# Two more projections by Strassen's seven products, with the residual kept token by token

## The chip, the cores and the metric

The kernel runs on one core of a Trainium2 chip. The core has a matrix engine (TensorE, PE in the profile), a vector engine (VectorE, DVE), an engine for activation functions and copies (ScalarE, ACT), GpSimd (POOL) and SyncE (SP), which here only issue transfers, and 16 DMA engines. Matmuls write PSUM, which has eight banks of 128 x 512 floats; all else lies in SBUF. The metric is the time of one execution on the device in microseconds (us).

## The reference

One layer of a decoder on 512 tokens of width 1024, all in float32, with 256 memory tokens:

```
h = x
h = h + hybrid_mixer(rmsnorm(h, mix_norm), ...)
h = h + memory_cross_attention(rmsnorm(h, xattn_norm), rmsnorm(mem, mem_norm), w_q, w_kv, w_o)
h = h + swiglu(rmsnorm(h, ffn_norm), w_gate_up, w_down)
return rmsnorm(h, final_norm)
```

The mixer ends in `concatenate([y_ssd, y_pool]) @ w_out`, where y_ssd (1024 channels) has a normalization of its own and y_pool (1024 channels) comes from causal pooling. The attention has four heads of 256 and ends in `o @ w_o`. Three 1024 x 1024 matrices matter here: the lower half of w_out, applied to y_pool (**op**); its upper half, applied to y_ssd (**os**); and w_o (**o**; its PSUM tile is called wo).

## The kernel before

**Precision.** A float32 product is made of three matmuls in a reduced format (fp32r): each operand is split into a high part, a cast by ScalarE, and a low part, the rest, a subtraction by VectorE. `mm3` issues high x high, high x low and low x high into one PSUM accumulation. Weights are split on the chip too: `split_unit` takes one loaded 128 x 1024 unit, casts it (line 203, tile whi) and subtracts (line 205, tile wlo).

**Two kinds of projection.** The plain kind (`proj`) holds one weight tile and streams 512 tokens: for one block m of 128 output channels, 8 input blocks times three matmuls. Its result has channels on partitions and tokens along the free axis. op, os, q and o are of this kind; `i_op(m)`, `i_os(m)` and `i_o(m)` make one block each, and add it to a residual that also has channels on partitions (xT, tiles `st["hp", m]` and `st["h1", m]`).

The other kind (`product`, line 1104) is Strassen's: both operands are cut in two by two blocks, seven sums of blocks ("forms" 1 to 7) are made on each side, and seven products are accumulated into three pairs of PSUM banks (A: forms 1, 6, 7, 4; B: 5, 3; C: 2), which are read out after each form. Here activations are the held operand and weights are streamed, so the result has tokens on partitions. The value part of w_kv, the gate/up matrix (g) and the down matrix (d) are done this way. Weight forms: for each chunk of 128 x 1024 blocks, forms 1, 2, 4 are loaded as they are (1 and 2 into the tiles of tags m and m2, which hold masks in the mixer; others into `wraw`), forms 5 and 7 are a load and a second load that POOL issues with addition, form 6 is an addition by a transfer that POOL issues, form 3 is an addition by VectorE (line 194). Activation forms are made by `forms`: four casts by ScalarE, and sums and low parts by VectorE.

**Turning.** q streams activations with channels on partitions, the FFN forms need them as well, and the FFN's output is added to a residual with tokens on partitions. So after o, `i_turn(r, c)` transposes the residual on PE, ScalarE copies it and squares it for the next normalization. The sums of squares for os and q are accumulated over blocks by VectorE, summed over partitions by a matmul with ones (`Rms`), and `i_r2t` transposes one of them.

**Order.** SPEC is a list of slots written by hand; each names items. P are the head pairs of the mixer, z and g its gate, v and p the pooling; k, q, V the projections of the attention, S scores, T the turned probabilities, O:h the output of head h; H the turned residual; U, Y, d the FFN's gate/up, turn and down. An item of a product names block, form and part: U:0.2.1 is block 0, form 2, second half of the inner sum; y:5.0 is form 5, first half. For each slot the kernel writes the evacuation (`post`) of the items of the slot before, the preparation (`prep`) of the items after, the splitting of weight units one slot ahead, and then the matmuls (`mm`). Past the first slot a planner orders each engine's list from these priorities, its own costs and the buffers that are free, so neighbours in SPEC interleave. Buffers: six PSUM tiles of one bank (tag ps) and one of two banks (tag pd), four whi, five wlo, six raw, 69 activation tiles of 128 x 512. SP issues loads in order; POOL issues the adding ones in order.

Of the kernel before, what the change touches and what calls it, by code (L numbers as in the profile page):

```python
# [61 lines left out]
def hybrid_block(ctx: ExitStack, tc: tile.TileContext, a: dict, out: bass.AP,  # L62
# [724 lines left out]
    def i_op(m):  # L787
        it = Item(keys=[("op", m)])

        def prep():  # L790
            it.x = T("x2")
            nc.sync.dma_start(it.x, a["xT"][m * P:(m + 1) * P, :])

        def mm():
            proj(hold(it, "op"), ready[("op", m)], [st["pg", k] for k in range(8)])

        def post():
            nc.vector.tensor_tensor(out=it.x, in0=it.x, in1=it.ps, op=ALU.add)
# [8 lines left out]

    def i_os(m):
        it = Item(keys=[("os", m)])

        def mm():
            proj(hold(it, "os"), ready[("os", m)], [st["yg", k] for k in range(8)])

        def post():
            t = mul("ot", it.ps, st["ry",])
            h = st["hp", m]
            nc.vector.tensor_tensor(out=h, in0=h, in1=t, op=ALU.add)
            st["h1", m] = h
            yield
            yield from splits([("hg", m)], [("hg", 512)], [h], col(V_XAT + m))  # L820
            if sq_acc("hacc", h):
                yield from rms2.split()
# [3 lines left out]


# [114 lines left out]
    def i_r2t():  # L942
        it = Item()

        def mm():
            pt = hold(it, "r2t")
            for c in range(NC):
                nc.tensor.transpose(pt[:, c * P:(c + 1) * P], st["r2",][:, c * P:(c + 1) * P], ident)

        def post():  # L950
            s = SM("r2s", [P, NC])
            nc.vector.tensor_scalar(out=s, in0=it.ps.rearrange("p (c l) -> p c l", l=P)[:, :, 0],
                                    scalar1=1.0 / 16.0, scalar2=None, op0=ALU.mult)
            st["r2s",] = s

        it.mm, it.post = mm, post
        return it

# [61 lines left out]
    def i_pv(h):  # L1020
# [19 lines left out]
    def i_o(m):  # L1040
        it = Item(keys=[("o", m)])

        def mm():
            proj(hold(it, "wo"), ready[("o", m)], [st["o", k] for k in range(8)])

        def post():
            h = st["h1", m]
            nc.vector.tensor_tensor(out=h, in0=h, in1=it.ps, op=ALU.add)
            yield
            i, c = m // 2, m % 2  # L1050
            if c == 0:
                st["F", i] = T("fa"), T("fb")
            for k in range(2):
                nc.scalar.activation(st["F", i][k][:, 256 * c:256 * c + 256], h[:, 256 * k:256 * k + 256],
                                     AF.Identity, scale=col(V_FFN + m))
            yield
            if c == 1:
                yield from forms("fg", i, *st["F", i])

        it.mm, it.post = mm, post  # L1060
# [154 lines left out]
    def i_turn(r, c):  # L1215
# [7 lines left out]

        def post():
            st["h", c, r] = T("hT")
            nc.scalar.copy(st["h", c, r], it.ps)
            if (r, c) == (0, 0):
                st["s3"] = small.tile([P, 32], F32, tag="s3", name="s3", bufs=1)
            nc.scalar.activation(T("sq"), st["h", c, r], AF.Square, accum_out=st["s3"][:, 4 * r + c:4 * r + c + 1])
            if (r, c) == (1, 3):  # L1230
                yield
                v, y, w, p, n = [st["s3"][:, o:o + 4] for o in (8, 12, 16, 20, 24)]
                nc.vector.tensor_tensor(out=v, in0=st["s3"][:, 0:4], in1=st["s3"][:, 4:8], op=ALU.add)
                nc.vector.tensor_scalar(out=v, in0=v, scalar1=1.0 / DM, scalar2=EPS, op0=ALU.mult, op1=ALU.add)
                nc.scalar.activation(y, v, AF.Ln)
                nc.scalar.activation(y, y, AF.Exp, scale=-0.5)
                nc.vector.tensor_tensor(out=w, in0=v, in1=y, op=ALU.mult)
                nc.vector.tensor_tensor(out=w, in0=w, in1=y, op=ALU.mult)
                nc.vector.tensor_scalar(out=w, in0=w, scalar1=-0.5, scalar2=1.5, op0=ALU.mult, op1=ALU.add)
                nc.vector.tensor_tensor(out=p, in0=w, in1=y, op=ALU.mult)  # L1240
                st["drained"] = nc.vector.tensor_scalar(out=n, in0=p, scalar1=-1.0, scalar2=None, op0=ALU.mult)
                st["nr3",], st["r3",] = n, p
# [316 lines left out]
```

## Time and profile before

| | us |
|---|---|
| median of 3 runs (lowest, highest) | 793.7 (793.55, 793.85) |
| the profiled execution | 794.94 |
| its span, first to last instruction | 793.1 |
| PE busy | 782.3 (99%) |
| VectorE busy | 635.4 (80%) |
| ScalarE busy | 499.6 (63%) |
| granted clock of PE | 0.997 of full |

A row of groups reads: line, engine, operation, output<-inputs, shapes, count | busy time, mean ns of one | idle time of that engine just before them, and what ended most of it. A row of a windows view has, for a stretch from A to B us, its length, the busy time (and count) of PE, of its weight loads PEld, of DVE, ACT and POOL, the granted clock, the share of the DMA engines and GB/s. A row of the chain of waits has start, length, engine and tile, and one of the timeline start, length, engine, line and operation; a matmul's length there is longer than the step to the next, because matmuls overlap.

### The profile page before, as it was taken

What the parts mean: (1) busy time and instruction counts of PE and PEld (TensorE: products, weight loads), DVE (VectorE), ACT (ScalarE), POOL (GpSimd) and SP (SyncE); (2) the same over time, 40 slices, a digit from 0 to 9 for tenths busy, and PEclk for the clock granted to TensorE, in tenths of its full rate; (3) what the DMA queues carried; (4) which work ended last, traced back from release to release, by engine and by line L of the source; (5) the groups of instructions that cost most, each with busy time, mean ns of one, the idle gap of its engine ahead of it and who ended that gap; (6) DMA issues with size and microseconds to landing.
All of it is one profiled execution on the core that took longest, in us unless ns stands there. A gap on an engine that the chain in (4) does not pass through costs nothing.

```text
span 793.1 us, 10458 instructions
## 1 busy us (share of the span) xinstructions
PE 782.3 (99%) x3789; PEld 655.9 (83%) x3789; DVE 635.4 (80%) x944; ACT 499.6 (63%) x803; POOL 49.8 (6%) x66
## 2 busy tenths in 40 slices
PE   9999999999999999999999999999999999999996
PEld 7878888888888888888888888888888888888984
DVE  7999879999895798875766667788857798867897
ACT  8667699657953547555655695665445575455855
POOL 0000000000000000000000011011101011101000
PEclk9999999999999999999999999999999999999998
DMA  9235326134474234765455268787869798879702
GB/s 336 86 110 177 114 86 179 54 105 127 158 262 161 93 107 149 171 188 165 132 126 145 68 142 232 173 242 160 250 143 297 162 248 181 239 157 264 177 14 106
DMA packets 41283, 128.60 MB, mean 162 GB/s; under 512 B 4865, under 2 KB 7297, under 8 KB 41233
## 3 DMA queue, kind: packets, MB, share of 16 engines
q1 hardware_dynamic: 32880, 99.04, 36.9%
q0 software_dynamic: 8064, 28.58, 20.2%
q8 instruction: 29, 0.48, 0.2%
q10 hardware_dynamic: 288, 0.33, 0.1%
q14 instruction: 22, 0.17, 0.1%
HBM read 116.63 MB, written 2.13 MB: 150 GB/s over the span
## 4 chain that ended last, share of the span: by engine, by line
PE 84%; DVE 9%; DMA 3%; ACT 2%; issue 2%; SPq 0%; DVEq 0%
PE gA L1104 14%; PE gB L1104 8%; PE dA L1104 4%; PE gC L1104 3%; PE dB L1104 2%; DVE wlo L205 2%; PE vAB L1104 2%; PE k L889 2%; DVE t_hT L1263 2%; PE op L117 2%; PE wo L119 2%; PE op L118 2%; PE wo L117 2%; PE q L118 2%; PE q L117 2%; PE os L118 2%
## 5 line engine op out<-in xcount | busy, mean ns | idle before, releaser
L203 ACT CAST whi<-raw 128x1024 fp32r<-128x1024 f32 (+1 forms) x125 | 129.0, 1040 | 90.6 <-PE wo L118 11.8
L205 DVE TENSOR_TENSOR wlo<-raw,whi 128x1024 fp32r<-128x1024 f32 (+1 forms) x125 | 150.0, 1208 | 28.2 <-ACT whi L203 27.3
L203 ACT CAST whi<-wq 128x1024 fp32r<-128x1024 f32 (+1 forms) x76 | 77.4, 1028 | 74.5 <-PE dA L1104 17.8
L205 DVE TENSOR_TENSOR wlo<-wq,whi 128x1024 fp32r<-128x1024 f32 (+1 forms) x76 | 90.3, 1194 | 38.8 <-ACT whi L203 38.6
L172 POOL DMA_DIRECT2D raw<-w_s x38 | 32.7, 865 | 646.4 <-DMA raw<-w_s 521.6
L1104 PE MATMUL gA<-whi,t_xh 128*128 128x512 f32 (+1 forms) x192 | 71.7, 373 | 0.0
L1104 PE MATMUL gA<-wlo,t_xh 128*128 128x512 f32 (+1 forms) x192 | 71.4, 372 | 0.0
L1104 PE MATMUL gA<-whi,t_xl 128*128 128x512 f32 (+1 forms) x192 | 71.3, 371 | 0.0
L1104 PEld LDWEIGHTS gA<-whi,t_xh 128*128 128x128 f32 x192 | 36.2, 188 | 6.3
L1104 PEld LDWEIGHTS gA<-wlo,t_xh 128*128 128x128 f32 x192 | 36.2, 188 | 6.3
L1104 PEld LDWEIGHTS gA<-whi,t_xl 128*128 128x128 f32 x192 | 36.2, 188 | 6.1
L1120 ACT ACTIVATE t_gu<-t_gu,s 128x512 f32<-128x512 f32 (+1 forms) x24 | 16.4, 687 | 34.9 <-DVE t_gu L1116 34.9
L194 DVE TENSOR_TENSOR wq<-wq,wq 128x1024 f32<-128x1024 f32 (+1 forms) x19 | 22.5, 1194 | 16.7 <-DMA wq<-raw 16.7
L1104 PE MATMUL dA<-whi,t_xh 128*128 128x512 f32 (+1 forms) x91 | 34.7, 385 | 0.5 <-DVE t_hT L1263 0.3
L1104 PE MATMUL dA<-whi,t_xl 128*128 128x512 f32 (+1 forms) x91 | 34.8, 382 | 0.0
L1104 PE MATMUL dA<-wlo,t_xh 128*128 128x512 f32 (+1 forms) x91 | 34.6, 382 | 0.0
L1104 PE MATMUL gB<-whi,t_xq 128*128 128x512 f32 (+1 forms) x96 | 27.6, 371 | 0.0
L117 PE MATMUL z<-t_uh,whi 128*128 128x512 f32 x64 | 25.2, 394 | 0.6 <-ACT t_uh L233 0.6
L1182 ACT CAST t_xh<-t_x 128x512 fp32r<-128x512 f32 x30 | 18.6, 621 | 10.6 <-DVE t_x L1201 6.4
L117 PE MATMUL wo<-t_oh,whi 128*128 128x512 f32 x64 | 25.2, 394 | 0.0
L117 PE MATMUL v<-t_uh,whi 128*128 128x512 f32 x64 | 25.1, 392 | 0.0
L117 PE MATMUL q<-t_hgh,whi 128*128 128x512 f32 x64 | 25.1, 392 | 0.0
(406 smaller groups left out, 2224.6 us busy)
## 6 DMA issues: line engine op xcount, KB each, us to landing
raw<-w_u SPq DMA_DIRECT2D x68, 512.0 KB, 3.4
raw<-w_s SPq DMA_DIRECT2D x54, 512.0 KB, 4.5
wq<-w_s SPq DMA_DIRECT2D x36, 512.0 KB, 5.6
raw<-w_s POOLq DMA_DIRECT2D x36, 512.0 KB, 7.1
wq<-raw POOLq DMA_DIRECT2D x17, 512.0 KB, 8.2
t_x<-xT SPq DMA_DIRECT2D x16, 256.0 KB, 5.3
t_abc<-d_acs SPq DMA_DIRECT2D x16, 256.0 KB, 5.1
out<-t_hT SPq DMA_DIRECT2D x7, 256.0 KB, 2.1
```

Source lines behind the costliest of these rows:

```text
L117: nc.tensor.matmul(ps, whi, xhi, start=start, stop=False)
L118: nc.tensor.matmul(ps, whi, xlo, start=False, stop=False)
L119: nc.tensor.matmul(ps, wlo, xhi, start=False, stop=stop)
L172: nc.gpsimd.dma_start(sw[c, f][:, :n], quad("11" if f == 7 else "22"), accum_op=ALU.add)
L194: add = nc.vector.tensor_tensor(out=sw[c, 3][:, :n], in0=sw[c, 3][:, :n], in1=sw[c, 6][:, :n], op=ALU.add)
L203: nc.scalar.copy(hi[:, :n], raw[:, :n])
L205: nc.vector.tensor_tensor(out=lo[:, :n], in0=raw[:, :n], in1=hi.bitcast(F32)[:, :n], op=ALU.subtract)
L889: nc.tensor.matmul(it.ps[d], wh[:, ws], both, start=k == 0, stop=False, skip_group_check=True)
L1104: nc.tensor.matmul(it.ps[tt][:, o:e], p[:, ts_], w[:, ws], start=first, stop=(c, i, n) == pairs[-1] and p is xh and w is wl, skip_group_ch ...
L1120: st["silu"] = nc.scalar.activation(g, g, AF.Silu, scale=st["r3",][:, c:c + 1])
L1182: nc.scalar.copy(h if w is None else h[:, w], src)
L1263: d = nc.vector.tensor_tensor(out=h[:, half], in0=h[:, half], in1=it.ps[tt][:, half], op=ALU.add if sign > 0 else ALU.subtract)
```

## The change

- **The residual has tokens on partitions from the start.** `i_op` loads x (not its transpose) into eight tiles h[c, r] (c one of 4 token tiles, r one of 2 halves of the channels), and every projection adds to them in place.
- **op stays plain but swaps operands:** activations are held, 512 output channels are streamed. Four items (k = 0 to 3) accumulate into four PSUM banks, one for each token tile; then four additions empty them, and four items do the other half.
- **os becomes y, o becomes o, both by `product`**, with two chunks each at the end of CHUNKS. Bank pair B of both is the two-bank tile pd. Their evacuations (`i_y`, `i_o`) add each form's pair of banks into h; `i_y` multiplies by the token's factor 1/rms in the same instruction, with its sign.
- **New activation forms:** `natural_forms` makes the seven forms from an even and an odd block, for the gated y (`i_yforms`), for the attention's heads (`i_pv`, which first copies both blocks out of PSUM) and for the FFN (`i_turn`), in place of `forms`; `forms` stays for the inside of the FFN.
- **Normalizations:** sums of squares come from ScalarE's accumulating squares of h (`i_squares`), or, for y, from a product of the accumulated squares with a column of ones (`i_ry`), and `rsqrt` works on 128 x 4 values. `Rms` for os and q, and `i_r2t`, go.
- **Turning:** `i_hg(m)` transposes h for q, and `i_turn(m)` for the FFN, four 128 x 128 transposes each.
- **Slots** around these are rewritten. Host packing of weights follows.

```diff
+CHUNKS += [(t, 0, ks, 512) for t in ("y", "o") for ks in ((0, 1), (2, 3))]
...
-    "P:7", "op:0 g:5 op:1 op:2 g:6", "op:6 g:4 op:3 g:7", "op:5 op:4 ys", "op:7 yr", "os:0 ml", "os:1", "os:2",
-    "os:3 mm", "os:4", "os:5", "os:6", "os:7", "k:0", "k:1 r2", "k:2 vf:0", "k:3 rt vf:1", "q:0 vf:2 vf:3", "q:1 V:1", "q:2 V:2",
-    "q:3 S:0 V:5", "q:4 V:6",  "q:5 S:1 T:0 V:3", "q:6 S:2 T:1", "q:7 V:7 T:2", "V:4 S:3 O:0", "O:1", "T:3 O:2", "O:3", "o:0", "o:1",
-    "o:2", "o:3", "o:4 H:0.0", "o:5 H:0.1", "o:6 H:0.2", "o:7 H:0.3",
-    "U:0.1.0 H:1.0 H:1.1", "U:0.2.0 H:1.2 H:1.3", "U:0.5.0", "U:0.1.1 U:0.2.1", "U:0.5.1", "U:0.6", "U:0.3", "U:0.7", "U:0.4",
+    "P:7", "op:0 g:5 op:1 op:2 g:6", "op:3 g:4 op:4 g:7 yf:0", "op:5 op:6 yf:1", "op:7 yf:2", "yr yf:3 ml", "y:1.0", "y:2.0", "y:5.0",
+    "y:1.1 y:2.1", "y:5.1 mm", "y:6", "y:3", "y:7 hg:0 hg:1", "y:4 hg:2 hg:3", "k:0", "k:1 hg:4 hg:5", "k:2 hg:6 hg:7 vf:0 sq:2.0",
+    "k:3 vf:1 sq:2.1", "q:0 vf:2 vf:3", "q:1 V:1", "q:2 V:2",
+    "q:3 S:0 V:5", "q:4 V:6",  "q:5 S:1 T:0 V:3", "q:6 S:2 T:1", "q:7 V:7 T:2", "V:4 S:3 O:0", "O:1", "o:1.0 T:3 O:2",
+    "o:5.0 O:3", "o:2.0", "o:1.1 o:2.1", "o:5.1", "o:6", "o:3", "o:7.0", "H:0 H:1 o:7.1", "H:2 H:3 o:4.0", "o:4.1",
+    "U:0.1.0 H:4 H:5", "U:0.2.0 H:6 H:7", "U:0.5.0", "U:0.1.1", "U:0.2.1", "U:0.5.1 sq:3.0", "U:0.6 sq:3.1", "U:0.3", "U:0.7", "U:0.4",
...
-                yield from splits([("yg", j)], [("yg", 512)], [y], col(V_SSD + j))
                 sq_acc("yacc", y)
+                nc.scalar.activation(y, y, AF.Identity, scale=col(V_SSD + j))
+                st["yg", j] = y
...
+    def i_op(j):
+        it = Item(keys=[("op", j)])
+        r, k = j // 4, j % 4
...
+            for c in (2 * j, 2 * j + 1) if j < 4 else ():
+                t = st["h", c % NC, c // NC] = T("h")
+                nc.sync.dma_start(t, a["x"][c % NC * P:c % NC * P + P, 512 * (c // NC):512 * (c // NC) + 512])
+
+        def mm():
+            if k == 0:
+                st["op"] = [PS("op") for _ in range(NC)]
...
+            for c in range(NC):
+                cs = slice(c * P, (c + 1) * P)
+                for n in range(2):
+                    ws = slice(512 * n, 512 * n + 512)
+                    xh, xl = st["pg", 2 * k + n]
+                    mm3(it.ps[c], xh[:, cs], xl[:, cs], wh[:, ws], wl[:, ws], k == 0 and n == 0, k == 3 and n == 1)
...
+    def i_ry():
...
+            ps = hold(it, "ry")
+            for c in range(NC):
+                nc.tensor.matmul(ps[:, c:c + 1], st["yacc"][:, c * P:(c + 1) * P], ones[:, 0:1], start=True, stop=True)
...
+    def i_y(f, part=None):
+        it, ends, _ = product("y", 0, f, part)
...
+                nc.vector.scalar_tensor_tensor(out=h, in0=it.ps[tt], scalar=st["ry",][sign][:, c:c + 1], in1=h,
+                                               op0=ALU.mult, op1=ALU.add)
...
+    def i_hg(m):
...
+            pt = hold(it, "hgT")
+            for c in range(NC):
+                nc.tensor.transpose(pt[:, c * P:(c + 1) * P], st["h", c, m // 4][:, (m % 4) * P:(m % 4 + 1) * P], ident)
+
+        def post():
+            yield from splits([("hg", m)], [("hg", 512)], [it.ps], col(V_XAT + m))
...
@@ i_pv
-            yield from splits([("o", 2 * h + d) for d in range(2)], [("o", 512)] * 2, it.ps)
+            E, O = T("oe"), T("oo")
+            nc.scalar.copy(E, it.ps[0])
+            nc.scalar.copy(O, it.ps[1])
+            yield
+            yield from natural_forms("of", h, E, O)
...
+    def i_o(f, part=None):
+        it, ends, _ = product("o", 0, f, part)
...
+                nc.vector.tensor_tensor(out=h, in0=h, in1=it.ps[tt], op=ALU.add if sign > 0 else ALU.subtract)
...
+    def natural_forms(x, i, E, O):
...
+        H1 = cast(E, a_)
+        HO = cast(O)
+        M = T("x57")
+        nc.vector.tensor_tensor(out=M[:, a_], in0=E[:, a_], in1=E[:, b_], op=ALU.subtract)
+        nc.vector.tensor_tensor(out=M[:, b_], in0=O[:, b_], in1=E[:, b_], op=ALU.subtract)
+        yield
+        rest(H1[:, b_], E[:, a_], H1[:, a_])
+        LO = T("xl", F32R)
+        rest(LO, O, HO)
...
+        H2 = cast(M)
+        N = T("x64")
...
+        H3 = cast(N)
+        L2 = T("xl", F32R)
+        rest(L2, M, H2)
...
+        L3 = T("xl", F32R)
+        rest(L3, N, H3)
...
+    def i_turn(m):
...
+            st["fgT", m] = T("fT")
+            nc.scalar.activation(st["fgT", m], it.ps, AF.Identity, scale=col(V_FFN + m))
+            yield
+            if m % 2:
+                yield from natural_forms("fg", m // 2, st["fgT", m - 1], st["fgT", m])
```

More of the change, by code (lines that the diff above doesn't have):

```diff
@@ L811, in mm, with square @@
+    def square(name, c, r):
+        if name not in st:
+            st[name] = small.tile([P, 8], F32, tag="s23", name=name, bufs=1)
+        nc.scalar.activation(T("sq"), st["h", c, r], AF.Square, accum_out=st[name][:, NC * r + c:NC * r + c + 1])
+    def i_ry():
+        it = Item()
         def mm():
-            proj(hold(it, "os"), ready[("os", m)], [st["yg", k] for k in range(8)])
+            ps = hold(it, "ry")
+            for c in range(NC):
+                nc.tensor.matmul(ps[:, c:c + 1], st["yacc"][:, c * P:(c + 1) * P], ones[:, 0:1], start=True, stop=True)
@@ L814, in post @@
         def post():
[L815 to L822, printed above, removed]
+            p, n = rsqrt("ry", it.ps[:, 0:NC])
+            nc.vector.tensor_scalar(out=n, in0=p, scalar1=-1.0, scalar2=None, op0=ALU.mult)
@@ new lines, in post @@
+            st["ry",] = {1: p, -1: n}
+        it.mm, it.post = mm, post
+        return it
+    def i_y(f, part=None):
+        it, ends, _ = product("y", 0, f, part)
+        def post():
+            yield from need("ry")
+            r, k, sign = INTO[f]
+            for tt in range(2):
+                c = 2 * k + tt
+                h = st["h", c, r]
+                nc.vector.scalar_tensor_tensor(out=h, in0=it.ps[tt], scalar=st["ry",][sign][:, c:c + 1], in1=h,
+                                               op0=ALU.mult, op1=ALU.add)
+                yield
+        it.post = post if ends else None
+        return it
@@ new lines, in i_squares, with prep @@
+    def i_squares(n, r):
+        def prep():
+            for c in range(NC):
+                square(f"s{n}", c, r)
+                yield
+            if r:
+                p, q = rsqrt(f"r{n}", st[f"s{n}"][:, 0:4], st[f"s{n}"][:, 4:8])
+                if n == 2:
+                    s = SM("r2s", [P, NC])
+                    nc.vector.tensor_scalar(out=s, in0=p, scalar1=1.0 / 16.0, scalar2=None, op0=ALU.mult)
+                    st["r2s",] = s
+                else:
+                    st["drained"] = nc.vector.tensor_scalar(out=q, in0=p, scalar1=-1.0, scalar2=None, op0=ALU.mult)
+                    st["nr3",], st["r3",] = q, p
+        return Item(prep=prep)
@@ L940, in i_q @@
         return it
[L942 to L957, printed above, removed]
     def i_score(h):
@@ L1034, in post @@
         def post():
-            yield from splits([("o", 2 * h + d) for d in range(2)], [("o", 512)] * 2, it.ps)
+            E, O = T("oe"), T("oo")
+            nc.scalar.copy(E, it.ps[0])
+            nc.scalar.copy(O, it.ps[1])
+            yield
+            yield from natural_forms("of", h, E, O)
         it.mm, it.post = mm, post
         return it
[L1040 to L1044, printed above, removed]
+    def i_o(f, part=None):
+        it, ends, _ = product("o", 0, f, part)
         def post():
[L1047 to L1060, printed above, removed]
+            r, k, sign = INTO[f]
+            for tt in range(2):
+                c = 2 * k + tt
+                h = st["h", c, r]
+                nc.vector.tensor_tensor(out=h, in0=h, in1=it.ps[tt], op=ALU.add if sign > 0 else ALU.subtract)
+                yield
+        it.post = post if ends else None
         return it
@@ L1220, in mm @@
             pt = hold(it, "hT")
-            for i in range(4):
-                nc.tensor.transpose(pt[:, i * P:(i + 1) * P], st["h1", 4 * r + i][:, c * P:(c + 1) * P], ident)
+            for c in range(NC):
+                nc.tensor.transpose(pt[:, c * P:(c + 1) * P], st["h", c, m // 4][:, (m % 4) * P:(m % 4 + 1) * P], ident)
         def post():
[L1225 to L1242, printed above, removed]
+            st["fgT", m] = T("fT")
+            nc.scalar.activation(st["fgT", m], it.ps, AF.Identity, scale=col(V_FFN + m))
+            yield
+            if m % 2:
+                yield from natural_forms("fg", m // 2, st["fgT", m - 1], st["fgT", m])
         it.mm, it.post = mm, post
@@ L1497, in _pack @@
     wo = g["w_out_mix"]
-    u += [mtile(wo[1024:], m) for m in range(8)]
-    u += [mtile(wo[:1024], m) for m in range(8)]
+    wp = wo[1024:].reshape(4, 2, P, 2, 512)
+    u += [wp[k, :, :, r].transpose(1, 0, 2).reshape(P, 1024) for r in range(2) for k in range(4)]
     wkv = g["w_kv"]
@@ L1502, in _pack @@
     u += [mtile(g["w_q"], m) for m in range(8)]
-    u += [mtile(g["w_o"], m) for m in range(8)]
     w_u = np.stack([f(t) for t in u])
```

87 lines of the change are left out of this document (61 added, 26 removed).

## The prediction

> **What bounds the kernel now.** I read the page first: busy shares, then the chain that ended last.
>
> ```profile
> span 793.1 us, 10458 instructions
> ...
> PE 782.3 (99%) x3789; PEld 655.9 (83%) x3789; DVE 635.4 (80%) x944; ACT 499.6 (63%) x803; POOL 49.8 (6%) x66
> ...
> PE 84%; DVE 9%; DMA 3%; ACT 2%; issue 2%; SPq 0%; DVEq 0%
> ```
>
> TensorE (PE) is busy 99% of the span and holds 84% of the chain; VectorE (DVE) is next at 80%. A busy PE may hide waits, since matmuls overlap, so I took the waits of PE and its step from the chain in order of time.
>
> ```profile
> PE warm L384 <- DVE ones L100: 1.2, 1, 1.2
> PE z L117 <- ACT t_uh L233: 0.6, 1, 0.6
> ...
> 484.93 16.32 PE gA L1104 x72
> 501.25 5.44 PE gC L1104 x24
> 506.69 0.88 PE ffT L1163 x8
> ```
>
> Only five waits are listed, none over 1.2 us. Full matmuls step by 5.44 / 24 = 0.2267 us, transposes by 0.88 / 8 = 0.11 us. The windows show whether other engines are near their limit where the change lands.
>
> ```profile
> core 0: us, PE busy (x) PEld busy (x) DVE busy (x) ACT busy (x) POOL busy (x), PEclk, DMA share, GB/s
> 150.00:200.00 50.00, 49.59 (x245) 41.67 (x244) 48.58 (x85) 32.48 (x61) 0.00 (x0) 1.00 0.30 92
> 200.00:320.50 120.50, 120.50 (x579) 101.36 (x578) 97.98 (x153) 73.93 (x120) 1.87 (x2) 1.00 0.48 158
> 398.00:485.00 87.00, 87.00 (x406) 71.91 (x405) 55.36 (x91) 55.91 (x105) 6.81 (x8) 1.00 0.52 131
> 410.00:432.00 22.00, 22.00 (x98) 18.21 (x98) 10.29 (x16) 8.56 (x15) 1.70 (x2) 1.00 0.37 99
> 600.00:654.00 54.00, 54.00 (x248) 44.87 (x247) 41.96 (x54) 32.35 (x43) 7.67 (x9) 1.00 0.86 231
> ```
>
> From 200 to 320.5 (op, os, k) and from 398 to 485 (attention values, wo, start of the FFN) PE never stops and DVE is idle 22.5 and 31.6 us. From 150 to 200 DVE is busy 97% and PE still loses only 0.41 us. So PE sets the time, and a matmul taken out is worth its step as long as DVE keeps up.
>
> **The change on PE.** os and wo have 8 x 8 x 3 = 192 matmuls each; seven products of 4 pairs x 2 token tiles x 3 are 168. That removes 2 x 24 x 0.2267 = 10.88 us. op keeps its 192, with operands exchanged: nothing. The turned copy of the residual for q (`i_hg`) adds 8 x 4 = 32 transposes, 32 x 0.11 = 3.52 us; the 32 of the FFN exist now and only stand elsewhere. The two sums of squares on PE go, two matmuls each, and the four transposes of `i_r2t`. A row of the chain and one of the timeline:
>
> ```profile
> 253.66 0.45 PE ry L299 x2
> ...
> 1.18 5.36 PE L384 MATMUL warm<-ones 128*128 128x128 f32 x24 [1.18 <-DVE ones L100]
> ```
>
> That is 2 x 0.45 + 4 x 0.11 = 1.34 us less. `i_ry` adds four f32 products one column wide, which the trace does not show. A f32 product is two passes (the 12 of warm are x24), so eight: between 8 x 0.11 = 0.88 us at the step of a transpose and 8 x 5.36 / 24 = 1.79 us at that of warm. I take 0.9, since warm runs at the start of the program and with 128 columns. Sum on PE: -10.88 + 3.52 - 1.34 + 0.9 = -7.8 us.
>
> **The change on DVE.** This is the cover on which that sum rests; the groups by shape give the prices.
>
> ```profile
> L205 DVE TENSOR_TENSOR wlo<-raw,whi 128x1024 fp32r<-128x1024 f32 x46 | 56.0, 1222 | 13.6 <-ACT whi L203 13.6
> L194 DVE TENSOR_TENSOR wq<-wq,wq 128x1024 f32<-128x1024 f32 x4 | 4.9, 1222 | 0.1
> L1186 DVE TENSOR_TENSOR t_xl<-t_x,t_xh 128x512 fp32r<-128x512 f32 x8 | 5.5, 689 | 0.3
> L1191 DVE TENSOR_TENSOR t_x<-t_fa,t_fb 128x256 f32<-128x256 f32 x4 | 1.7, 418 | 0.0
> L1048 DVE TENSOR_TENSOR t_x<-t_x,wo 128x512 f32<-128x512 f32 x8 | 5.5, 685 | 18.0 <-PE wo L119 18.0
> L241 DVE TENSOR_TENSOR t_ol<-o,t_oh 128x512 fp32r<-128x512 f32 x8 | 5.4, 689 | 2.5 <-ACT t_oh L233 2.4
> L329 DVE TENSOR_TENSOR t_ot<-os,t_ryt 128x512 f32<-128x512 f32 x8 | 5.5, 689 | 2.9 <-PE os L119 2.8
> L817 DVE TENSOR_TENSOR t_x<-t_x,t_ot 128x512 f32<-128x512 f32 x8 | 5.5, 691 | 0.2
> L324 DVE TENSOR_TENSOR t_hacc<-t_hacc,t_sq 128x512 f32<-128x512 f32 x7 | 4.8, 688 | 0.1
> L243 DVE SCALAR_TENSOR_TENSOR t_ygl<-t_y,vec,t_ygh 128x512 fp32r<-128x512 f32 x4 | 3.0, 748 | 0.1
> L311 DVE SCALAR_TENSOR_TENSOR t_ryt<-ry,eps,t_ryy 128x512 f32<-128x512 f32 x1 | 0.8, 751 | 2.2 <-ACT t_ryy L308 2.2
> L292 DVE TENSOR_TENSOR t_ryl<-t_yacc,t_ryh 128x512 fp32r<-128x512 f32 x1 | 0.7, 685 | 0.0
> L1233 DVE TENSOR_TENSOR s<-s 128x4 f32<-128x4 f32 x1 | 0.2, 164 | 1.9 <-ACT t_sq L1229 1.9
> ```
>
> wo stage, 398 to 485: 14 weight units for 8 are 6 more low parts (7.3), two form-3 sums are 2.4. Each `natural_forms` is 5 half operations of 0.42 and 3 whole of 0.69, 4.2 us; four for the heads are 16.7, and the 8 low parts of o (5.5) go. 14 updates of h for 8 add 6 x 0.685 = 4.1. The FFN forms keep their number. Together +25.0 us, against 31.6 idle less the 5.4 by which PE's stage shrinks: 26.2. It fits by 1.2 us.
>
> os stage, 200 to 320.5: the same 7.3 + 2.4 + 16.7; 14 updates at 0.75 (10.5) for a multiplication and an addition on 8 tiles (11.0): -0.5; the four yg low parts that lie there -3.0, the sum of squares -4.8, the two wide reciprocal roots -5.6 (a low part and three of about 0.7 each), their narrow successors 13 x 0.16 = +2.1. Together +14.6, against 22.5 less 2.4: 20.1 us. It fits by 5.5. So I cost DVE at nothing on PE's path, but in the wo stage this rests on using nearly all its idle time.
>
> **ACT and DMA.** In the wo stage ACT gets 6 casts of weights, 16 casts in the forms, 8 copies:
>
> ```profile
> L203 ACT CAST whi<-raw 128x1024 fp32r<-128x1024 f32 (+1 forms) x125 | 129.0, 1040 | 90.6 <-PE wo L118 11.8
> L1182 ACT CAST t_xh<-t_x 128x512 fp32r<-128x512 f32 x30 | 18.6, 621 | 10.6 <-DVE t_x L1201 6.4
> ```
>
> At most 6.2 + 24 x 0.62 = 21.1 us, on 55.9: 77 of 81.6 even if nothing went. Hidden. Each new chunk is seven loads of 0.5 MB instead of four, three of its forms being added up by transfers that POOL issues: some 4 MB more per stage, 131 GB/s to about 190. From 600 to 654, products of this kind run at 231 GB/s with PE at 54.00 of 54. Hidden too. The new h loads are 8 as the xT loads were, on SP, two per item.
>
> The answer for the line of POOL's accumulating loads shows what its issues cost now.
>
> ```profile
> L172 POOL DMA_DIRECT2D raw<-w_s x38: 844/857/1072, 314.8 to 738.9; - x38
> ...
> DMA to landing us min/median/max: 5.1/7.1/10.1
> ```
>
> [...]
>
> **Waits that may be new.** Three places, each bounded by zero and a row.
>
> First, op. It now takes four of the six PSUM banks at once, where one item took one. The timeline at its start, PE first, then DVE and ACT:
>
> ```profile
> 206.95 0.45 PE L117 MATMUL op<-t_pgh,whi 128*128 128x512 f32 x1
> ...
> 211.29 0.28 PE L119 MATMUL pd<-mh,t_xcl 128*128 128x256 f32 x1
> ...
> 210.69 0.56 DVE L696 TENSOR_TENSOR t_E<-yo,t_E 128x384 f32<-128x384 f32 x1 [1.49 <-ACT t_E L653]
> ...
> 214.99 0.60 ACT L711 ACTIVATE t_z<-z 128x512 f32<-128x512 f32 x1
> ...
> 219.96 0.74 DVE L243 SCALAR_TENSOR_TENSOR t_pgl<-po,vec,t_pgh 128x512 fp32r<-128x512 f32 x1
> ```
>
> When op starts at 207, yo, z and both po banks are still held; the third is free at 211.2, the fourth at 215.6. op:0 alone reaches its fourth token tile at 207 + 3 x 6 x 0.2267 = 211.1: up to 4.5 us. But P:7's 12 half-width matmuls and op:1 and op:2 on the first three tiles can be put between. 0 to 4.5; I take 0.5. Behind it PE's whole list waits. The same stretch frees the two mask tiles that the first two forms of y are loaded into: P:7's last product is over at 211.6, and y:1.0 comes about 40 us later, so that wait, and SP's loads queued behind it, cost nothing.
>
> Second, o:1.0 stands right behind O:1, whose output must be copied, cast and reduced (two copies and a half cast on ACT, a half low part on DVE): 2 x 0.62 + 0.4 + 0.42 + handovers, 2.6 us, less the 0.68 of its first pair. T:3 and O:2 are behind it and can be drawn ahead. 0 to 1.9; I take 0.5. Third, U:0.1.1 needs the forms of H:6 and H:7 one part (2.72 us) after they are turned, the same chain: 0 to 2; I take 0.5.
>
> Sum: -7.8 + 1.5 = -6.3. The profiled execution took 794.94 us (1.84 outside its span, unchanged); it becomes 788.6. It lies 1.24 above the median of the runs, so I forecast 787.4.
>
> **Rivals.**
> A. The banks at op bind fully: -7.8 + 4.5 + 1.0, 791.4. For it: ACT holds z until 215.6 today. Against it: it has had no reason to let go sooner.
> B. The forms come late at both places: -7.8 + 3.9 + 0.5, 790.3.
> C. Slower. DVE becomes the bound of the wo stage, because its idle time is not where the work is: from 410 to 432 it sat 22 - 10.3 = 11.7 us, waiting for evictions of wo. If the new forms cannot fill that stretch, since they come in chains behind O:0 to O:3 and the H turns, DVE overruns by 11.7 - 1.2 = 10.5 us, and PE waits for low parts and updates: -7.8 + 10.5, 796.4. It decides from 7.8 + 1.2 = 9.0 us of unusable idle time. For it: 98% is asked of DVE. Against it: the 97% row above cost 0.41 us, and weight low parts can be made some units ahead.
> D. POOL's transfers come late: 7.1 to 10.1 us, 3.0 for each of four new chunks and nothing covering it: 787.4 + 12 = 799.4. [...]
>
> **How the numbers follow.** Forecast 0.55, own range 785.5 to 790; A 0.10, B 0.10, C 0.21, D 0.04. No change means within 0.2% (1.6 us), about what this kernel's runs can tell. C is graded: a third of it ends within that, the rest slower. Faster 0.55 + 0.10 + 0.10 = 0.75, same 0.07, slower 0.14 + 0.04 = 0.18. The range runs from no new wait (793.7 - 7.8 = 785.9, and half a microsecond) to C's price: 785.4 to 796.5.
>
> **What would show it.** 168 matmuls each into y and o; PE without gaps over 1 us at op's fourth tile, o:1.0 and U:0.1.1; DVE near 95% in the wo stage while the waits of PE for DVE stay under 2 us in all. Wrong if PE waits for `wlo`, for h updates or for `t_xl` by more than 6 us between the attention and the first FFN block, or if PE's busy time falls by clearly less than 7 us.

## The result and the profile after

The changed kernel takes 800.6 us (median of 4 runs, 799.58 to 801.54) against 793.78 us for the kernel before beside it: a ratio of 1.0083, 95% interval 1.0068 to 1.0098. It is slower by 0.8%, and outside the forecast range of 785.4 to 796.5. The profiled execution took 800.07 us.

The page of the changed kernel: span, busy time of each engine, and the chain that ended last by engine.

```profile
span 798.4 us, 10584 instructions
...
PE 778.7 (98%) x3773; PEld 649.6 (81%) x3773; DVE 663.8 (83%) x1009; ACT 516.2 (65%) x837; POOL 60.1 (8%) x78
...
PE 76%; DVE 14%; DMA 3%; issue 3%; ACT 3%; SPq 0%; POOL 0%; DVEq 0%; POOLq 0%; ACTq 0%
```

PE's share of the chain fell from 84% to 76%, and DVE's rose from 9% to 14%. PE has 16 matmuls fewer, as the change says (48 and 4 and 4 out, 32 and 8 in). So the work went, and PE now waits for something. Where it waits is seen from the start of each product's first matmul. In the answers for a tile the last pair of numbers is the start of the first and of the last instruction. Before, the tiles of the gate product (gA) and the down product (dA):

```profile
L1104 PE MATMUL gA<-whi,t_xh x192: 277/389/481, 455.4 to 755.8; 128*128 128x512 f32 x160, 128*128 128x256 f32 x32
L1104 PE MATMUL dA<-whi,t_xh x91: 278/389/504, 535.5 to 785.0; 128*128 128x512 f32 x85, 128*128 128x256 f32 x6
```

The same two of the changed kernel:

```profile
L1173 PE MATMUL gA<-whi,t_xh x240: 277/389/797, 449.7 to 760.4; 128*128 128x512 f32 x100, 128*128 128x256 f32 x20
L1173 PE MATMUL dA<-whi,t_xh x91: 278/389/497, 540.6 to 789.6; 128*128 128x512 f32 x85, 128*128 128x256 f32 x6
```

The FFN starts 5.7 us earlier, as hoped. But from gA to dA, the FFN's first two blocks, it takes 90.9 us in place of 80.1: 10.8 us are lost in a stage whose matmuls the change doesn't touch. After it nothing more is lost (dA to its last matmul: 249.0 after, 249.5 before). Windows of 5 us in that stage, of the kernel before:

```profile
450.00:455.00 5.00, 5.00 (x23) 4.08 (x22) 1.93 (x3) 2.61 (x7) 0.00 (x0) 1.00 0.30 105
455.00:460.00 5.00, 5.00 (x29) 4.27 (x28) 4.18 (x8) 5.00 (x10) 1.71 (x2) 1.00 0.53 86
```

and of the changed kernel:

```profile
450.00:455.00 5.00, 2.25 (x11) 1.43 (x9) 3.64 (x5) 1.19 (x2) 0.00 (x0) 1.00 0.09 17
455.00:460.00 5.00, 3.54 (x12) 2.75 (x12) 5.00 (x10) 2.18 (x3) 0.42 (x1) 0.66 0.32 105
...
470.00:475.00 5.00, 4.12 (x18) 3.39 (x19) 4.97 (x10) 4.32 (x7) 0.86 (x1) 1.00 0.27 32
475.00:480.00 5.00, 5.00 (x24) 4.14 (x23) 2.12 (x5) 5.00 (x17) 0.00 (x0) 1.00 0.92 274
480.00:485.00 5.00, 4.89 (x21) 3.31 (x19) 2.12 (x7) 4.97 (x9) 0.00 (x0) 1.00 0.22 68
```

In the first two, PE is idle for 2.75 and 1.46 us, and its granted clock in the second is 0.66, so that up to half of the 3.4 us that it ran slow (456.0 to 459.4, at 0.50) is lost as well. The DMA share of the first is 0.09: hardly anything was being moved. From 480 to 485 PE looks 4.89 us busy, but did 21 matmuls where the window before it has 24. The timeline shows who was late, DVE first, then PE.

```profile
446.24 0.42 DVE L1311 SCALAR_TENSOR_TENSOR t_x<-t_x,t_fT 128x256 f32<-128x256 f32 x1
451.36 1.23 DVE L196 TENSOR_TENSOR wq<-wq,wq 128x1024 f32<-128x1024 f32 x1 [4.70 <-DMA wq<-raw]
452.50 1.29 DVE L1294 TENSOR_TENSOR t_xl<-t_x,t_xh 128x512 fp32r<-128x512 f32 x2
453.70 0.68 DVE L1123 TENSOR_TENSOR t_h<-t_h,oA 128x512 f32<-128x512 f32 x1
...
451.31 0.39 PE L1173 MATMUL gA<-whi,t_xh 128*128 128x512 f32 x1
454.44 0.44 PE L1330 MATMUL hT<-ident,t_h 128*128 128x128 f32 x2 [2.75 <-DVE t_h L1123]
```

DVE stood for 4.70 us at a form-3 weight sum (line 196), waiting for a transfer that POOL issues. The sum belongs to the FFN's first block; its product comes some 30 us later (gB from 481.91). But behind it in DVE's list stood the last updates of the residual, which PE's next turn needed. The same sum in the kernel before, with the next update of the residual:

```profile
445.49 1.23 DVE L194 TENSOR_TENSOR wq<-wq,wq 128x1024 f32<-128x1024 f32 x1
...
449.51 0.68 DVE L1048 TENSOR_TENSOR t_x<-t_x,wo 128x512 f32<-128x512 f32 x1
```

It stood at a like place, ahead of residual updates, and waited for nothing. So what changed for this sum is the transfer. POOL's timeline has its issue, before and after:

```profile
439.81 0.85 POOL L211 DMA_DIRECT2D wq<-raw  x1 [9.73 <-DVE wlo L205]
```

```profile
442.31 0.85 POOL L213 DMA_DIRECT2D wq<-raw  x1 [1.73 <-DVE wlo L207]
```

Against the start of gA (455.4 and 449.7) that is 15.6 us ahead before and 7.4 after: the FFN starts earlier and the issue, behind a low part by DVE, comes later. Before, it landed within 5.7 us, since the sum ran at 445.49; after, 9.05 us passed from the issue to the sum. Such a landing isn't new: over the whole span those of this line go from 3.3 to 11.7 us (median 7.8) before and from 4.0 to 11.2 (median 7.9) after.

The block's second sum came to wait for another reason. `split_unit` puts a form-3 sum behind an instruction that was noted by the time form 5 was split (`sw[c, "drained"] = st.get("drained")`). Before, the turn of the last residual tile, at the slot of U:0.2.0, notes the last step of its reciprocal root, in time for the second sum (for the first, nothing is noted in either kernel). After, that root is made by `i_squares(3, 1)` at the slot of U:0.6, too late, and the planner puts the sum where its costs allow. DVE and PE of the changed kernel:

```profile
467.39 1.23 DVE L196 TENSOR_TENSOR wq<-wq,wq 128x1024 f32<-128x1024 f32 x1 [2.11 <-DMA wq<-raw]
...
470.41 0.42 DVE L1294 TENSOR_TENSOR t_xh<-t_fT,t_xh 128x256 fp32r<-128x256 f32 x1
...
470.88 0.50 PE L1173 MATMUL gA<-whi,t_xh 128*128 128x512 f32 x1 [1.04 <-DVE t_xh L1294]
```

DVE's waits for such transfers over the whole span went from 16.7 us to 26.6, as the group rows before and after say:

```profile
L194 DVE TENSOR_TENSOR wq<-wq,wq 128x1024 f32<-128x1024 f32 (+1 forms) x19 | 22.5, 1194 | 16.7 <-DMA wq<-raw 16.7
```

```profile
L196 DVE TENSOR_TENSOR wq<-wq,wq 128x1024 f32<-128x1024 f32 (+1 forms) x23 | 27.4, 1198 | 26.6 <-DMA wq<-raw 26.6
```

A second place is ScalarE's, in the timeline of the changed kernel:

```profile
474.68 0.64 ACT L850 ACTIVATE t_sq<-t_h 128x512 f32<-128x512 f32 x1
...
478.99 0.62 ACT L850 ACTIVATE t_sq<-t_h 128x512 f32<-128x512 f32 x1
...
479.60 0.57 ACT L1195 COPY t_gu<-gB 128x512 f32<-128x512 f32 x1
```

Eight squares in a row, 4.9 us, hold the copies out of gB and the casts of weights behind them. Before, each square was written behind the copy of its own turn.

How the 10.8 us are made up is seen from PE's starts: what lies between two of them beyond a matmul's step (0.2267 us, or 0.11 for a transpose) is lost. From gA to dA that is 11.2 us after and 0.5 before. An estimate by place, from these starts: 6.0 at the first sum with the slow clock behind it (451 to 460), 1.3 at the second sum, 1.5 where the copies out of gB are held (481 to 487), 1.0 at the wait of gB for t_fT (466) and 1.0 at a wait of gA for t_gu (534).

### The profile page after: what moved, and what is told of

Same layout as the page of the kernel before. It is cut to its first block, busy times and chain, and to the rows that moved or that the text cites. A ratio compares the mean times of both kernels' runs of the same rounds, so it can differ in the third digit from the quotient of the medians.

```text
span 798.4 us, 10584 instructions
## 1 busy us (share of the span) xinstructions
PE 778.7 (98%) x3773; PEld 649.6 (81%) x3773; DVE 663.8 (83%) x1009; ACT 516.2 (65%) x837; POOL 60.1 (8%) x78
## 4 chain that ended last, share of the span: by engine, by line
PE 76%; DVE 14%; DMA 3%; issue 3%; ACT 3%; SPq 0%; POOL 0%; DVEq 0%; POOLq 0%; ACTq 0%
PE gA L1173 13%; PE gB L1173 6%; PE dA L1173 5%; DVE wlo L207 3%; PE gC L1173 3%; PE dB L1173 2%; PE yA L1173 2%; PE xbc L120 2%; PE xbc L119 2%; PE xbc L121 2%; PE vAB L1173 2%; DMA wq<-raw 2%; PE k L977 2%; PE z L119 2%; PE z L120 2%
## 5 line engine op out<-in xcount | busy, mean ns | idle before, releaser
L205 ACT CAST whi<-wq 128x1024 fp32r<-128x1024 f32 (+1 forms) x92 | 94.2, 1032 | 81.6 <-PE dA L1173 17.8
L207 DVE TENSOR_TENSOR wlo<-wq,whi 128x1024 fp32r<-128x1024 f32 (+1 forms) x92 | 109.6, 1196 | 38.4 <-ACT whi L205 38.1
L1173 PE MATMUL gA<-whi,t_xh 128*128 128x512 f32 (+1 forms) x240 | 82.7, 376 | 3.3 <-DVE t_xh L1294 2.5
L1173 PE MATMUL gA<-whi,t_xl 128*128 128x512 f32 (+1 forms) x144 | 53.5, 371 | 0.0
L196 DVE TENSOR_TENSOR wq<-wq,wq 128x1024 f32<-128x1024 f32 (+1 forms) x23 | 27.4, 1198 | 26.6 <-DMA wq<-raw 26.6
L1189 ACT ACTIVATE t_gu<-t_gu,r 128x512 f32<-128x512 f32 (+1 forms) x24 | 16.3, 687 | 34.0 <-DVE t_gu L1185 34.0
L1173 PE MATMUL gB<-whi,t_xh 128*128 128x512 f32 (+1 forms) x96 | 36.3, 378 | 1.0 <-ACT t_fT L1334 0.7
L1173 PE MATMUL gB<-wlo,t_xh 128*128 128x512 f32 (+1 forms) x96 | 35.6, 374 | 0.1
L1173 PE MATMUL gB<-whi,t_xl 128*128 128x512 f32 (+1 forms) x96 | 35.7, 372 | 0.0
L213 POOL DMA_DIRECT2D wq<-raw x22 | 19.8, 902 | 81.4 <-DVE wlo L207 62.9
L119 PE MATMUL op<-whi,t_pgh 128*128 128x512 f32 x64 | 25.1, 393 | 0.2 <-DVE t_h L822 0.2
```

The costliest lines, as they stand in the source:

```text
L119: nc.tensor.matmul(ps, whi, xhi, start=start, stop=False)
L196: add = nc.vector.tensor_tensor(out=sw[c, 3][:, :n], in0=sw[c, 3][:, :n], in1=sw[c, 6][:, :n], op=ALU.add)
L205: nc.scalar.copy(hi[:, :n], raw[:, :n])
L207: nc.vector.tensor_tensor(out=lo[:, :n], in0=raw[:, :n], in1=hi.bitcast(F32)[:, :n], op=ALU.subtract)
L213: nc.gpsimd.dma_start(sw[c, 6][:, :n], sw[c, 5][:, :n], accum_op=ALU.add)
L1173: nc.tensor.matmul(it.ps[tt][:, o:e], p[:, ts_], w[:, ws], start=first, stop=(c, i, n) == pairs[-1] and p is xh and w is wl, skip_group_ch ...
```

## The experiments

The theories were these. Order: the loss is the place of the form-3 sums in DVE's list, ahead of work that could go while their transfers are on the way. Squares: it is the eight squares in a row on ScalarE. Raw tiles: the transfers come late for want of `wraw` buffers. Load (rival C): DVE simply has too much to do.

**Order alone, in the first FFN block.** The last update of h and the last low part of the FFN's forms are noted, so that the sums come behind them.

```diff
+                d = nc.vector.tensor_tensor(out=h, in0=h, in1=it.ps[tt], op=ALU.add if sign > 0 else ALU.subtract)
+                if f == 4:
+                    st["drained"] = d
...
+        if x == "fg":
+            st["drained"] = st["last rest"]
```

> The two form-3 sums of the first FFN block are placed behind the last updates of the residual (first chunk) and behind the turned forms (second chunk) in VectorE's list; nothing else is changed. Theory ORDER (VectorE stands in front of a sum whose transfer has not landed, and the residual updates, low parts and then PE queue behind it): the wait of 4.7 us in front of the sum at 451 shrinks below 1.5 us, PE's wait for t_h of 2.7 us goes, the granted clock stays at 1.0 from 450 to 465, and the time falls by 5 to 8 us to 793 to 796. Theory LOAD (VectorE has too much to do in this stage): all its work stays, so the time moves by less than 1.5 us. Theory TRANSFERS (the data themselves are late): the wait moves to the later place of the sum and PE waits for wlo instead; less than 3 us.

793.38 us (792.66 to 796.23), ratio to the kernel before 0.9996 (0.9987 to 1.0006): 7.2 us won back by the place of two instructions. The wait of hT is gone, and the clock stays at 1.00 from 450 to 465. The profiled execution is the slowest of the ten (796.23), so the largest waits left in it (those for wlo lie behind 500) need not be those of the others:

```profile
PE gB L1175 <- DVE wlo L207: 2.3, 2, 1.5
PE gB L1175 <- ACT t_fT L1338: 1.3, 1, 1.3
```

**Order in y and o as well** (the same note after every set of natural forms).

> As the run before, and the form-3 sums of the two new projections are placed behind the low parts of their activation forms as well. Theory ORDER: the 1.6 us wait before y begins goes; 0 to 2 us less than the run before, 791 to 795. Theories LOAD and TRANSFERS: no difference to the run before within 1 us, or somewhat slower since sums come later.

794.39 us, 1.0011 (0.9999 to 1.0023): nothing more is won; the sums of y and o, which the change added, cost PE nothing where they are.

**Squares.** The first four go to the slot of o:4.1, the others to U:0.5.0.

```diff
-"o:4.1",
+"o:4.1 sq:3.0",
-"U:0.5.0", "U:0.1.1", "U:0.2.1", "U:0.5.1 sq:3.0", "U:0.6 sq:3.1",
+"U:0.5.0 sq:3.1", "U:0.1.1", "U:0.2.1", "U:0.5.1", "U:0.6",
```

> Only the slots of the sums of squares for the FFN are moved: the first half two slots ahead of U:0.1.0, the second half beside U:0.5.0, so that ScalarE does them between the casts of the forms instead of eight in a row at 474.7 to 479.6. Theory SQUARES (this run of 4.9 us holds up the copies of gB and the casts of weights): 1.5 to 3 us faster, 797.5 to 799. Theory ORDER alone: within 1 us of 800.6, since the wait in front of the sum stays.

797.45 us, 1.0046 (1.0029 to 1.0063): 3.1 us won. The wait of hT stayed, 2.5 us, and so did the slow clock:

```profile
450.00:455.00 5.00, 2.32 (x10) 1.18 (x8) 3.97 (x5) 1.85 (x4) 0.00 (x0) 1.00 0.05 8
455.00:460.00 5.00, 3.75 (x12) 3.05 (x13) 5.00 (x11) 2.18 (x3) 0.77 (x2) 0.66 0.31 105
```

So the stall at 450 is the order's. But this edit moves more than the squares: `i_squares(3, 1)` makes the root that is noted, the note now comes in time for the second sum, and DVE does that sum at 470.21, right behind the root, without a wait. By PE's starts, the 1.5 us at the copies out of gB, the 1.3 at the second sum and the 1.0 at t_gu came back, and 0.7 was lost anew at t_fT (a wait of 1.4 for 0.7). So the squares are a second loss, but only about half of the 3.1 us is shown to be theirs.

**Raw tiles alone.** Eight buffers for `wraw` in place of six, four activation tiles fewer.

```diff
-act_bufs=69, la=1, wb=(6, 4, 5)
+act_bufs=65, la=1, wb=(8, 4, 5)
```

> Two more tiles for loaded weights (8 for 6), paid with four activation tiles (65 for 69); order rules as in the changed kernel. Theory TRANSFERS (the chunks of o hold the tiles that the first FFN chunks are loaded into, so their sums are late): the transfer of the first sum starts earlier than 442 and VectorE's wait in front of it shrinks to under 2 us; 3 to 7 us faster, 794 to 798. Theory LOAD: within 1 us, or slower if activation tiles run short. Theory ORDER alone: the sum is still placed early, but waits as long as the transfer is late: less than 2 us faster unless the transfer starts earlier.

798.12 us, 1.0056 (1.0039 to 1.0073). Some 2.5 us, and the wait of hT still 2.0 us. The transfer was issued no earlier (442.74 for 442.31), and DVE's wait in front of the sum shrank from 4.70 to 3.97 us only, so neither the earlier start nor the wait under 2 us of that theory came, and its time was missed by 0.1. Of the gain, 0.7 us lies at the wait of hT and 1.0 at the wait for t_gu, which is gone.

**Order and squares.**

> Both single edits together: form-3 sums of the first FFN block behind the residual updates and forms, and the FFN's sums of squares moved two slots ahead. The first alone gave 793.4 (7.2 less), the second 797.4 (3.1 less). Theory ORDER plus SQUARES (two separate places, 450 to 465 and 474 to 490): the gains add up, 789.5 to 791.5, and PE is dense from 450 to 490 but for the wait for the turned forms. Theory ONE PLACE (both act on the same stall): 792.5 to 794.

793.07 us, 0.9982 (0.9974 to 0.9991): hardly more than order alone, so the two gains (7.2 and 3.1) don't add up; one reason is that both edits mend the second sum. PE's timeline shows a new wait in the place of the old ones:

```profile
461.86 0.50 PE L1175 MATMUL gB<-whi,t_xh 128*128 128x512 f32 x1 [2.16 <-ACT t_fT L1338]
...
463.71 0.63 PE L1175 MATMUL gB<-whi,t_xh 128*128 128x512 f32 x1
464.14 0.63 PE L1175 MATMUL gB<-whi,t_xl 128*128 128x512 f32 x1
```

PE waits for the turned copies of H:6 and H:7, which must leave their bank before gB can have it, and then steps by 0.43 us (463.71 to 464.14) in place of 0.2267; the granted clock is 0.50 from 463 to 466. In ScalarE's timeline of the same run, the copies stand behind squares:

```profile
460.51 0.63 ACT L850 ACTIVATE t_sq<-t_h 128x512 f32<-128x512 f32 x1
...
461.14 1.24 ACT L1338 ACTIVATE t_fT<-hT,vec 128x512 f32<-128x512 f32 x2
```

**With eight raw tiles too.**

> As the run before with 8 tiles for loaded weights and 65 activation tiles. Theory TRANSFERS (what is left is the wait for sums that arrive late): 1 to 3 us less than the run before, 787 to 790. If the order was all: no difference within 1 us.

794.71 us, 1.0001 (0.9991 to 1.0012). That is 1.6 us more than without them, which neither theory had; the wait for t_fT is 2.1 us as before.

**Order everywhere, and squares.**

> As the first of this set, and the form-3 sums of the two new projections behind their activation forms too. With the first FFN block's order alone this addition did not show (794.4 against 793.4). Theory ORDER: the sum before y and the two at the attention values cost little, since PE has work then: within 1 us of the first of this set.

792.17 us, 0.9981 (0.9972 to 0.999), with the same 2.1 us wait for t_fT.

**Load.** The changed kernel without the 28 low parts of y's and o's weights; the high part stands in for each.

```diff
+        skip = key[0] == "s" and CHUNKS[c][0] in "yo"
+        lo = hi if skip else wlo_p.tile([P, 1024], F32R, tag="lo", name=nm("wlo"))
...
+        if not skip:
+            nc.vector.tensor_tensor(out=lo[:, :n], in0=raw[:, :n], in1=hi.bitcast(F32)[:, :n], op=ALU.subtract)
```

> The changed kernel with the 28 low parts of the weights of y and o left out (the high part stands in for them, so PE's work is the same); the form-3 sum still stands ahead of the last residual updates in VectorE's list. 28 x 1.14 = 32 us of VectorE's work go, 14 x 1.14 = 16 of them in the o stage. Theory LOAD (VectorE has too much to do): the whole loss goes, 786 to 789. Theory ORDER: the sum waits for its transfer as before, 797 to 801.

796.53 us, 1.0033 (1.0021 to 1.0046): half a microsecond outside the times of the theory of order, 7.5 outside those of load. The tile rows show where the 4.1 us went:

```profile
L1175 PE MATMUL gA<-whi,t_xh x240: 278/389/793, 447.4 to 756.6; 128*128 128x512 f32 x100, 128*128 128x256 f32 x20
L1175 PE MATMUL dA<-whi,t_xh x91: 277/389/497, 536.8 to 785.8; 128*128 128x512 f32 x85, 128*128 128x256 f32 x6
```

2.3 us are won ahead of gA, and from gA to dA it is still 89.4 us. With some 33 us (28 x 1.2) of DVE's work gone, 9.3 of the 10.8 us lost in the FFN stay: load is not the main cause. It has a small share: the first sum's transfer was issued 7.1 us ahead of gA (440.28), no earlier than the 7.4 above, but the sum came 6.83 us behind the issue in place of 9.05, DVE's wait in front of it was 2.52 us in place of 4.70, and PE's wait of hT fell from 2.7 to 0.8.

**Order everywhere, and the second four squares later,** at U:0.1.1, behind the copies of H:6 and H:7.

```diff
-"U:0.5.0 sq:3.1", "U:0.1.1",
+"U:0.5.0", "U:0.1.1 sq:3.1",
```

> Edit: all form-3 weight sums of y, o and the first FFN block ordered behind the forms or updates, the first four squares at o:4.1 as in the run with 792.17 us, the second four moved from U:0.5.0 to U:0.1.1. SQUARES-AHEAD: in that run TensorE waited 2.1 us at 460 for the bank that the turned copies of H:6 and H:7 free, and those copies (t_fT) stood on ScalarE behind four squares (3.3 us); the granted clock then was 0.81 and 0.85 from 460 to 470, which costs another 1.7 us. With the squares behind the copies the wait falls below 1 us, the clock stays at 1.00, and the time is 788 to 790. CHAIN: the copies are late by the chain of forms on VectorE, not by the squares: the wait stays over 1.5 us and the time within 1 us of 792.2.

790.92 us (790.34 to 791.13), 0.9957 (0.9944 to 0.9969): faster than both kernels, though 0.9 us above the times expected. PE's largest waits, and a window:

```profile
PE warm L386 <- DVE ones L102: 1.2, 1, 1.2
PE gB L1175 <- ACT t_fT L1337: 0.6, 1, 0.6
```

```profile
460.00:465.00 5.00, 4.71 (x19) 3.60 (x20) 4.97 (x11) 4.69 (x12) 0.00 (x0) 1.00 0.92 192
```

The wait fell from 2.1 to 0.6 us and the clock stays at 1.00. The squares ahead of the copies were the cause of that wait.

**The second four later still,** at U:0.2.1.

> As the run beside it, with the second four squares at U:0.2.1, the last place before the reciprocal root is needed. SQUARES-AHEAD: the same 788 to 790, or up to 1.5 us more if the additions of the first products, which need the root, come late and hold gC's bank. CHAIN: 791 to 794.

791.5 us, 0.9965 (0.9951 to 0.9978): the same within the intervals. The time fits both theories, but the wait for t_fT is 0.6 us here too, as only the first had it.

**The kernel before without its note,** so that its second form-3 sum moves up in DVE's list.

```diff
-                st["drained"] = nc.vector.tensor_scalar(out=n, in0=p, scalar1=-1.0, scalar2=None, op0=ALU.mult)
+                nc.vector.tensor_scalar(out=n, in0=p, scalar1=-1.0, scalar2=None, op0=ALU.mult)
```

> The kernel before with one edit: the last step of its reciprocal root no longer counts as the instruction behind which the first FFN block's form-3 sum is ordered, so that this sum stands about a dozen instructions earlier in VectorE's list, ahead of the forms of the last residual tiles. ORDER-ALONE: the sum waits for its transfer there too (over 1 us idle of VectorE on wq from raw before the first FFN block's second half), and the time rises by 2 us or more. ORDER-WITH-LATE-LOAD: in the kernel before the transfers are done early enough, the sum doesn't wait and the time stays within 1 us of 793.8; the changed kernel loses because its transfers also come later.

793.86 us, 0.9997 (0.9988 to 1.0006): no difference. The sum went from 471.23 to 463.35 and did wait:

```profile
445.02 1.23 DVE L194 TENSOR_TENSOR wq<-wq,wq 128x1024 f32<-128x1024 f32 x1
463.35 1.23 DVE L194 TENSOR_TENSOR wq<-wq,wq 128x1024 f32<-128x1024 f32 x1 [2.50 <-DMA wq<-raw]
```

Neither theory of this run foresaw that: the sum waited, which the first expected, and the time stayed, which the second did. That wait of 2.50 us in DVE's list cost nothing (793.86 us, and 793.93 for the kernel before beside it): PE's longest wait in the FFN of this run is 0.3 us (dA for t_hT). So the missing note does no harm by itself; it does with the changed kernel's list and its later transfers. How much each of the two sums cost was not run by itself either; the shares above (6.0 and 1.3 us) are from PE's starts. Why the first sum's transfer took longer to land was not tried; from its issue to the sum the DMA engines were busy for 0.48 of their time before and for 0.94 after.

## Why the prediction was wrong, point by point

- **The sum on PE, -7.8 us: its mechanism held, somewhat smaller.** The matmul count is exact, and at gA the gain is 5.7 us where -7.8 plus the first two waits (1.0) would have -6.8; the rest was lost in waits, below. `i_ry`, bounded by 0.88 and 1.79 and taken as 0.9, measured 0.9 (a row for it: eight passes). The test that was named, PE's busy time down by 7, was a bad one: it went from 782.3 to 778.7, since a busy PE includes slow clock (from 457 to 459 it is busy for 2.00 us with 6 matmuls, at a clock of 0.50) and gaps that the modelled ends cover (the 4.89 us with 21 matmuls from 480 to 485).

```profile
L858 PE MATMUL ry<-ones,t_yacc 128*128 128x1 f32 x8 | 0.9, 239 | 0.0
```

- **DVE at nothing on PE's path: the step that failed.** The total was checked against the idle time of a stage, and the total fits: in the stage of wo, costed at 55.4 + 25.0 = 80.4 us, the best version shows 73.8 of 82.7 (the row below). What wasn't checked is the order in DVE's list, where one instruction that waited for a transfer, 4.70 us at the first sum, held all behind it. And the working kept to what the change adds; the sums that stalled exist in both kernels. The step needed a sum of its own: the FFN was to start 6 us earlier, the first sum's transfer had 15.6 us ahead of it, and the landings of POOL's loads that the prediction quotes go up to 10.1; so the cover shrank to the length of a landing even before the issue came later. And the code that noted the root was taken out of `i_turn` in plain sight; what else orders itself by that note was not looked up.

```profile
395.90:478.60 82.70, 81.96 (x371) 65.31 (x371) 73.84 (x127) 60.36 (x108) 7.81 (x9) 1.00 0.61 154
```

- **Three new waits, 1.5 us in all: the list was short.** op's banks cost 0.5 by the starts of op and ry (46.6 us before, 47.1 after), as taken; around o:1.0, where 0.5 was taken, the listed waits are 0.3 (oB for t_xl) and 0.6 us (o for t_Pl), and by PE's starts from 402.06 to 412.86 it lost 1.5 us, inside the bounds of 0 to 1.9 (37 full matmuls and 8 transposes in 10.8 us, where 37 x 0.2267 + 8 x 0.11 = 9.3); the third, the turned tiles of H:6 and H:7, showed once the order was mended, as 2.2 us for t_fT: over the upper bound of 2 rather than 0.5, though by the copies that must free a bank and not by the forms. Missing were the two sums (2.75, 1.46 and 1.04 us of idle PE, and the clock), the squares (about 1.5), and 0.8 in the stage of y, where the sum of squares of the memory (rm) was late (1.7 us from 270.37 for matmuls worth 0.9).
- **Rival A** fell with its 0.5 us. **Rival B** named two places where PE did lose, 1.5 us around o:1.0 and 1.0 at U:0.1.1, the latter behind the second sum; it was not the main loss.
- **Rival C** had the right sign and the right engine, and the wrong mechanism: it spoke of DVE's amount of work. Without 28 of DVE's subtractions the FFN stage still lost 9.3 of 10.8 us.
- **Rival D** had POOL's transfers come late, by 3.0 us in each of the four new chunks. POOL's issues hardly got longer in the changed kernel, with DVE at 83%: 46 of them took 844 to 1002 ns (38 took 844 to 1072 before, with DVE at 80%), and the 22 of the line that feeds the sums 846 to 1195, with a median of 859 (18 took 846 to 864 before, with a median of 852). The first sum's transfer did land late, 9.05 us after the issue, though the kernel before has such landings too (up to 11.7). But the rival looked for that in the four new chunks of y and o, and it came in the FFN's first block; mending DVE's order, with nothing done to the transfers, took 7.2 us off, so the cost lies in what is queued behind them.

```profile
L174 POOL DMA_DIRECT2D raw<-w_s x46: 844/857/1002, 223.6 to 743.5; - x46
```

- **The margin.** With order and squares mended the kernel takes 790.9, 3.5 us above the forecast of 787.4. Half of that is between the profiled executions (790.34, where 788.6 was expected); the other half is that the forecast took off 1.24 us for the distance of a profiled execution to the median, and this one lies 0.58 below its median. By the starts of the products in that run, 1.7 us are lost from the first matmul of the attention values (tile o) to gA (53.5 us, where 57.2 - 5.44 = 51.8 was to be had), 1.0 in the stage of y (41.1 us, where 43.8 - 5.44 + 16 x 0.11 = 40.1 was), and 1.3 in the FFN's first two blocks (81.4 us for 80.1); op starts 1.2 us earlier than before, which no term has. PE's waits of that run don't show the 1.7, but its starts do: 35 full matmuls and 8 transposes from 401.78 to 411.88, where o's first forms stand among the attention values, take 10.1 us for 35 x 0.2267 + 8 x 0.11 = 8.8. One of the short pauses:

```profile
403.79 0.48 PE L1175 MATMUL oB<-whi,t_xh 128*128 128x512 f32 x1
404.40 0.50 PE L1175 MATMUL oB<-whi,t_xl 128*128 128x512 f32 x1
```

  So most of it is the second of the three new waits, taken as 0.5 and 1.3 in this run. What each pause waited for is not shown.

## What to carry to other kernels

An idle total says whether work fits on an engine; whether it delays another is decided by its list: here the total fitted, and one wait of 4.70 us in DVE's list became 2.75 of PE's. For each instruction that waits for a transfer, look up what stands behind it in the list and when that is needed, also for instructions that the change doesn't touch: a stage that starts earlier has less cover for its transfers (7.4 us in place of 15.6 here). When a change moves the place where a handle is noted, search for everything that orders itself by it. And spread a burst of small work (eight squares, 4.9 us) behind the copies that free a bank, not ahead of them: that took PE's wait from 2.1 to 0.6 us.

## What the runs showed of the hardware

A stall of PE cost more than its length here. In the changed kernel the step went to 0.43 us behind the two pauses between 451 and 457 (2.75 and 1.46 us); windows of 1 us there, with PE alone (length, busy time and count, granted clock, DMA share, GB/s), show the granted clock halved:

```profile
456.00:457.00 1.00, 0.42 (x1) 0.51 0.52 119
457.00:458.00 1.00, 1.00 (x3) 0.50 0.96 356
458.00:459.00 1.00, 1.00 (x4) 0.50 0.13 49
459.00:460.00 1.00, 1.00 (x7) 0.79 0.00 0
```

These four lack 0.49 + 0.50 + 0.50 + 0.21 = 1.70 us of full clock. At half, that is about 3.4 us, and it costs up to another 1.7, an estimate from these windows. With order and squares mended, the same followed one pause of 2.16 us: steps of 0.43 us, and a clock of 0.50 from 463 to 466. With order everywhere it followed one of 2.1 us, with a clock of 0.81 from 460 to 465 and 0.85 from 465 to 470. With eight raw tiles too, which has a pause of 2.1 us as well, only the mean clock of the profiled execution, 0.995, speaks for it. With the second four squares moved, a pause of 0.61 us left the clock at 1.00, and so did, with order alone, one of 1.25 us (460) and one of 1.47 (505). What decides it is not shown. With the 1.7 us, the wait of 2.16 us cost up to 3.9, again an estimate. By the mean granted clock it doesn't fall in each execution: with order everywhere and squares, that mean was 0.995 in five of the eleven executions, which took 793.26 to 794.24 us, and 0.997 in six, which took 791.16 to 792.17; 0.002 of 792 us is 1.6, about the price above. The profiled one (793.99) is of the five and the median (792.17) of the six, so the 1.25 us from that median to the best kernel's are not the price of the clock.
